# Within-chunk state-space kernels from a 32-column stationary operand, and the first loads in order of use

## The chip, the cores and the metric

One core of one Trainium2 chip runs the whole program. The metric is device time in microseconds (us), the median of several runs; less is better. The engines are TensorE (PE in the profile, its weight loads PEld), VectorE (DVE), ScalarE (ACT), GpSimd (POOL) and SyncE (SP, which here only sends DMAs). All work is in float32, or in pairs of float32r numbers that add up to one float32.

## What is computed

One layer of a hybrid encoder on a sequence of 512 tokens, width 2048, batch 1. The parts that the change touches are the input projection for `u` and the S5 scan; the rest is cut short.

```python
h = rmsnorm(x, norm_g)
v, bg, cg, za, u, zb, ga, gb = split(h @ w_in)      # 2048 -> 14336 columns
ya = (bg * causal_conv3(cg * v) * silu(za)) @ w_out_a
yb = gelu(s5_scan(u, ...))                          # 64 groups of 16 channels, 64 complex states each
yb = (yb * sigmoid(yb @ w_glu + b_glu) * silu(zb)) @ w_out_b
m = sigmoid(ga) * ya + sigmoid(gb) * yb
out = rmsnorm(x + m @ w_o, final_g)

# s5_scan, per group: lam_bar = exp(lam*dt); b_bar = (lam_bar-1)/lam * b
# h[l] = lam_bar * h[l-1] + b_bar @ u[l];  y[l] = Re(c @ h[l]) + d_skip * u[l]
```

## The kernel before

**Matrices.** Every large product is split: a float32 operand becomes a high part in float32r (an ACT cast, line 663 for weights, 734 for activations) and a low part (a DVE subtraction, line 680 for weights, 66 or 76 for activations), and PE sums hi·hi, hi·lo and lo·hi. The class `WStream` holds the order of all weight tiles: `_loads` sends the DMAs on the SP queue (line 641), `_hi` casts, `_lo` subtracts, `prep` does one weight's `_lo` and keeps the casts a little ahead, and `get` hands out the next pair after preparing up to two further ones. Most tiles in SBUF come from one pool of 37 slots, `r4`.

**Order of the stages.** First the projection for `u`: for each of 16 blocks k of 128 input channels, the block `x_k` (line 845) and the weight `w_k` (line 641) are loaded, `scale_x(k)` multiplies `x_k` by the norm's gain and splits it (line 893 on ACT, 76 on DVE), and 21 matmuls follow (lines 910 to 912). Squares for the norm (line 856) and, from k=2, steps of the state-space parameters (`ssm_params`, which loads them in line 91) go along. Then come the other projections, with the rest as background work. The list `bg` holds generators; after each product `step` runs some of them, so their instructions are written between the products. [...]

**The state-space blocks.** `ssm_blocks` treats the 64 groups in four blocks of 16 groups, 8 pairs each. A chunk is T = 4 steps, so there are 128 chunks in 512 tokens. The class `Block` has these stages:

- `loads`: the block's `u` in the layout [step and channel, chunk] (`u4`), and its parameters.
- `front`: `F`, the output matrix times powers of lam_bar for 0 to 4 steps (partitions are the 128 states of a pair of groups), and `bb`, the input matrix. Before, `bb` is two tiles of [128, 8 pairs, 4 steps, 2 groups, 16 channels], real and imaginary, in which the same 32 columns of a pair stand four times, once for each step. POOL clears them (line 344) and ACT fills them (line 347).
- `pe1`: line 376 gives each chunk's contribution to the states; lines 381 to 385 (shown in the profile as line 383) give the kernels within a chunk, `kp`: for each pair, `bb` is the stationary operand (128 states by 128 columns) and `F` for 0 to 3 steps the moving one (64 columns). `kp` therefore holds on each of four groups of 32 partitions the same numbers.
- `post`: copies the states' part out (line 394) and builds `mi`, the 128x128 matrix from the inputs of a chunk to its outputs: for step s, partitions 32s to 32s+31, the kernels for 0 to 3-s steps go to the outputs s to 3 (line 405, an ACT copy with the mask `msk`, which lets one group's 16 rows of every 32 through).
- `scan`: the recurrence over chunks on DVE; `pe2` (lines 484 and 487): outputs from `mi` and the states; `result` adds the skip part and writes to `uy`.

After the four blocks `gelu` forms the inputs of the GLU product. From there to the end come the GLU, both output projections (with products of 2x2 blocks in seven instead of eight multiplications, lines 1067 and 1072) and the last projection (line 1290).

Of the kernel before, what the change touches and what calls it, by code (L numbers as in the profile page):

```python
# [12 lines left out]
AF = mybir.ActivationFunctionType  # L13
# [3 lines left out]
P = 128  # L17
L = 512
D = 2048
KD = D // P  # L20
NG, NP, NC = 64, 64, 16
NQ = NG // 2
NB = 4
QB = NQ // NB
T = 4
# [55 lines left out]
def ssm_params(c, par, scratch):  # L81
# [3 lines left out]
    nc = c.nc  # L85
    tt, ts, stt = _ew(nc)
    W = 96
    a_t = c.r4.tile([P, 3, W], F32, tag="r4", name="ssm_par")
    keep = c.r4.tile([P, 14, 2, NQ], F32, tag="r4", name="ssm_keep")
    pw, up, coef, mag = keep[:, 0:5], keep[:, 5:12], keep[:, 12], keep[:, 13, 0]  # L90
    nc.gpsimd.dma_start(a_t, par)
    views = []

    def new():
        if not views:
            blk = c.r4.tile([P, 10, W], F32, tag="r4", name="ssm_tmp")
            views.extend(blk[:, i, :] for i in range(9, -1, -1))
        return views.pop()
# [94 lines left out]
    p1r, p1i, t = new(), new(), new()  # L193
# [51 lines left out]
    bt = c.r4.tile([P, 2, NQ, 8], F32, tag="r4", name="ssm_bt")  # L245
# [27 lines left out]
class Block:  # L273
# [32 lines left out]
    def front(self):  # L306
        c, nc, b, q0, msk = self.c, self.c.nc, self.b, self.q0, self.msk
        tt, ts, stt = _ew(nc)
        smal, wb, bs = self.smal, self.wb, self.bs

        self.F = []
        cr, ci = smal[:, :, 1, 0, :], smal[:, :, 1, 1, :]
        shp = [P, QB, NC]
        ft = self.new([P, QB, 5, NC], "ft")
        sh5 = [P, QB, 5, NC]
        p5 = [c.pw[:, :, i, q0:q0 + QB].rearrange("p t q -> p q t").unsqueeze(3).to_broadcast(sh5)
              for i in range(2)]
        c5 = [v.unsqueeze(2).to_broadcast(sh5) for v in (cr, ci)]
        for ri in range(2):
            f = self.new(sh5, "f")  # L320
            tt(ft, c5[1], p5[1 - ri], MUL)
            tt(f, c5[0], p5[ri], MUL)
            yield
            if ri == 0:
                tt(f, f, ft, SUB)
            else:
                fl = f.rearrange("p q t c -> p (q t c)")
                stt(fl, fl, -1.0, ft.rearrange("p q t c -> p (q t c)"), MUL, SUB)
            self.F.append(f)
            yield  # L330

        br, bi = smal[:, :, 0, 0, :], smal[:, :, 0, 1, :]
        kr = c.coef[:, 0, q0:q0 + QB].unsqueeze(2).to_broadcast(shp)
        ki = c.coef[:, 1, q0:q0 + QB].unsqueeze(2).to_broadcast(shp)
        self.bb = bb = [self.new([P, QB, T, 2, NC], "bb") for _ in range(2)]
        bt = [ft[:, :, i, :] for i in range(4)]
        tt(bt[0], br, kr, MUL)
        tt(bt[1], bi, ki, MUL)
        tt(bt[2], br, ki, MUL)
        tt(bt[3], bi, kr, MUL)  # L340
        tt(bt[0], bt[0], bt[1], SUB)
        tt(bt[2], bt[2], bt[3], ADD)
        for ri in range(2):
            nc.gpsimd.memset(bb[ri], 0.0)
            for g2 in range(2):
                hp = slice(g2 * 64, (g2 + 1) * 64)
                nc.scalar.copy(bb[ri][hp, :, :, g2, :],
                               bt[2 * ri][hp].unsqueeze(2).to_broadcast([64, QB, T, NC]))
        yield

        self.sl = []
        tmp = self.new([P, QB, 2, NP], "t")
        for ri in range(2):
            if ri == 0:
                tt(tmp, wb, bs, MUL)
                tt(tmp[:, :, 0, :], tmp[:, :, 0, :], tmp[:, :, 1, :], SUB)
            else:
                tt(tmp[:, :, 0, :], wb[:, :, 0, :], bs[:, :, 1, :], MUL)
                tt(tmp[:, :, 1, :], wb[:, :, 1, :], bs[:, :, 0, :], MUL)
                tt(tmp[:, :, 0, :], tmp[:, :, 0, :], tmp[:, :, 1, :], ADD)  # L360
            yield
            m = self.new([P, QB, 2, NP], "sl")
            for g2 in range(2):
                nc.scalar.activation(m[:, :, g2, :], tmp[:, :, 0, :], AF.Copy, scale=msk[:, g2:g2 + 1])
            self.sl.append(m)
            yield

    def pe1(self):
        c, nc = self.c, self.c.nc
        self.hp = []  # L370
        for ri in range(2):
            for half in range(2):
                ps = c.psum()
                for i in range(4):
                    q = half * 4 + i
                    nc.tensor.matmul(ps[:, i * NCH:(i + 1) * NCH],  # L376
                                     self.sl[ri][:, q].rearrange("p g s -> p (g s)"),
                                     self.u4[:, q, :], start=True, stop=True)
                self.hp.append(ps)
        kp = self.kp = c.psum()  # L380
        for q in range(QB):
            for ri in range(2):
                nc.tensor.matmul(kp[:, q * 64:(q + 1) * 64],  # L383
                                 self.bb[ri][:, q].rearrange("p t g c -> p (t g c)"),
                                 self.F[ri][:, q, 0:T].rearrange("p t c -> p (t c)"),
                                 start=ri == 0, stop=ri == 1)

    def post(self):
        c, nc, msk = self.c, self.c.nc, self.msk
        self.hs = []  # L390
        for ri in range(2):
            h = self.new([P, QB, NCH], "h")
            for half in range(2):
                nc.scalar.copy(h[:, half * 4:half * 4 + 4, :].rearrange("p q k -> p (q k)"),
                               self.hp[ri * 2 + half])
            self.hs.append(h)
            yield

        mi = self.mi = self.new([P, QB, T, 2, NC], "mi")
        nc.gpsimd.memset(mi, 0.0)  # L400
        kv = self.kp.rearrange("p (q t c) -> p q t c", t=T, c=NC)
        for s in range(T):
            hp = slice(s * 32, (s + 1) * 32)
            for g2 in range(2):
                nc.scalar.activation(mi[hp, :, s:T, g2, :], kv[hp, :, 0:T - s, :], AF.Copy,
                                     scale=msk[hp, g2:g2 + 1])
            if s % 2:
                yield

        self.el = []  # L410
        for ri in range(2):
            e = self.new([P, QB, T, 2, NC], "el")
            nc.gpsimd.memset(e, 0.0)
            for g2 in range(2):
                hp = slice(g2 * 64, (g2 + 1) * 64)
                nc.scalar.copy(e[hp, :, :, g2, :], self.F[ri][hp, :, 1:5, :])
            self.el.append(e)
            yield
# [278 lines left out]
def hybrid_kernel(ctx: ExitStack, tc: tile.TileContext, xT, x, cvec, fg, wu, wu7, wabc,  # L697
                  wgz, wgb, wga, wo, par, bs_d, be_d, ce_d, out):
    nc = tc.nc
    tt, ts, stt = _ew(nc)  # L700
    act = nc.scalar
    c = Ctx()
# [26 lines left out]
    def pair():  # L729
        t = c.r4.tile([P, 2, L], F32R, tag="r4", name="pair")  # L730
        return t
# [5 lines left out]
    W = WStream(c, 2, 2)  # L737
# [20 lines left out]
    for j in range(0, KD, 2):  # L758
        for i in range(4):
            W.add7(wabc[j, i, 0], wabc[j + 1, i, 0], wabc[j + 1, i, 1], wabc[j, i, 1])  # L760
        i = NAB + j - 2
# [18 lines left out]
    bgl, dsk, msk = cv_t[:, 64:72], cv_t[:, 72:104], cv_t[:, 104:106]  # L780
# [60 lines left out]
    def load_x(k):  # L841
        if k % 2 == 0:
            xt = c.r4.tile([P, 2, L], F32, tag="r4", name="xt")
            xs.extend([xt[:, 0], xt[:, 1]])
        nc.sync.dma_start(xs[k], xT[:, k])
# [13 lines left out]
    hp = []  # L859
# [27 lines left out]
    def scale_x(k):  # L887
        if k < KD:
            xg = pair()
            if k == 0:  # L890
                ts(xg[:, 0], xs[k], ng[:, k:k + 1], MUL)
            else:
                act.activation(xg[:, 0], xs[k], AF.Copy, scale=ng[:, k:k + 1])
            stt(xg[:, 1], xs[k], ng[:, k:k + 1], xg[:, 0].bitcast(F32), MUL, SUB)
            xgs.append(xg)

    load_x(0)
    W._loads(0)
    load_x(1)
    load_x(2)  # L900
    for k in range(KD):
        for i in range(2 * k + 3, min(2 * k + 5, KD)):
            load_x(i)
        xg = xgs.pop(0)
        hi, lo = W.get()
        for i in ((1, 2) if k == 0 else (k + 2,)):
            scale_x(i)
        for m in range(7):
            cs = slice(m * P, (m + 1) * P)
            nc.tensor.matmul(pu[m], hi[:, cs], xg[:, 0], start=k == 0, stop=False)  # L910
            nc.tensor.matmul(pu[m], hi[:, cs], xg[:, 1], start=False, stop=False)  # L911
            nc.tensor.matmul(pu[m], lo[:, cs], xg[:, 0], start=False, stop=k == KD - 1)  # L912
        for i in range(2 * k, min(2 * k + 2, KD)):
            square(i)
        if k >= 8:
            for _ in range(2):
                next(nrm, None)
        elif k >= 2:
            step(PRATE)
# [63 lines left out]
    for m in range(8):  # L983
        ps = psum()
        gemm(ps, yg)
        th, g = tmp(), tmp()
# [150 lines left out]
    for j in range(0, KD, 2):  # L1137
# [7 lines left out]
        i = NAB + j - 2  # L1145
# [40 lines left out]
    for j in range(NP7):  # L1186
# [5 lines left out]
        g, t = (v[:, j % 2] for v in mq[j // 2])  # L1192
# [322 lines left out]
```

## Time and profile before

| | |
|---|---|
| median of 3 runs | 1662.81 us (1661.98 to 1663.66) |
| the profiled execution | 1664.87 us, span 1663.1 us |
| PE busy | 1648.4 us, 99% of the span |
| DVE, ACT, POOL busy | 1289.0, 793.3, 226.5 us |
| matmuls of line 383 | 128 records, from 165.6 to 335.7 us |
| the first stage, 0 to 20 us | PE busy 16.51 us, DMA at 338 GB/s |

[...] A float32 matmul stands as two records. A wait is put down to the instruction that came last by the profile. "Idle before" stands in brackets behind a timeline row, with what ended it.

### The profile page before, as it was taken

The page shows a single profiled execution, that of the slowest core. Times are in us where ns is not written, and L with a number is a line of the kernel's source. Part 1 is how long each engine was busy: PE and PEld are TensorE (multiplying, and loading weights), DVE is VectorE, ACT ScalarE, POOL GpSimd, SP SyncE. Part 2 cuts the span into 40 slices and gives each one's busy share as a digit, 9 for nine tenths or more (in the row PEclk, how much of TensorE's full clock was granted, in tenths as well). Part 3 has the DMA queues.
Part 4 walks back from the last instruction along what each step waited for, and adds up shares of the span by engine and source line. Part 5 has one row for each costly group of instructions (what it writes and reads, how often), then busy time and mean ns, then how long its engine had stood idle before and what let it go on. Part 6 is the DMA issues. An engine that isn't in the chain of part 4 may idle for free.

```text
span 1663.1 us, 22776 instructions
## 1 busy us (share of the span) xinstructions
PE 1648.4 (99%) x8636; PEld 1415.5 (85%) x8636; DVE 1289.0 (78%) x1743; ACT 793.3 (48%) x1081; POOL 226.5 (14%) x352
## 2 busy tenths in 40 slices
PE   9999999999999999999999999999999999999997
PEld 7888888888888888888888888888888888888886
DVE  7897787885765687877778777777878688888497
ACT  6434455446422355545445555544545544445334
POOL 0003332200021100110110101001010221122000
PEclk9999999999999999999999999999999999999999
DMA  8323453442364567777777777777676888997683
GB/s 308 106 90 113 121 151 118 137 134 77 124 224 133 165 180 204 189 202 206 206 202 183 205 194 199 206 194 219 181 211 181 293 260 240 272 324 250 231 328 101
DMA packets 91822, 318.50 MB, mean 192 GB/s; under 512 B 11904, under 2 KB 12032, under 8 KB 91712
## 3 DMA queue, kind: packets, MB, share of 16 engines
q1 hardware_dynamic: 58608, 204.50, 35.7%
q0 software_dynamic: 32384, 111.45, 28.6%
q8 instruction: 67, 1.10, 0.3%
q10 hardware_dynamic: 720, 1.10, 0.2%
q14 instruction: 43, 0.35, 0.1%
HBM read 287.51 MB, written 25.30 MB: 188 GB/s over the span
## 4 chain that ended last, share of the span: by engine, by line
PE 91%; DMA 3%; DVE 2%; ACT 2%; issue 1%; POOL 0%; SPq 0%; DVEq 0%; ACTq 0%; POOLq 0%
PE ps L1067 33%; PE ps L1072 17%; PE ps L1290 9%; PE ps L835 8%; PE ps L834 8%; PE ps L833 8%; DMA h_sum<-yag 2%; PE ps L910 1%; PE ps L911 1%; PE ps L912 1%; PE ps L376 1%; PE ps L383 1%; PE ps L487 1%; DMA uy<-ssm_y 1%; DMA w_raw<-in_wga_dram 0%
## 5 line engine op out<-in xcount | busy, mean ns | idle before, releaser
L663 ACT CAST w_hi<-w_raw 128x1024 fp32r<-128x1024 f32 (+2 forms) x459 | 479.0, 1044 | 664.0 <-PE ps L1067 269.8
L680 DVE TENSOR_TENSOR w_lo<-w_raw,w_hi 128x1024 fp32r<-128x1024 f32 (+2 forms) x459 | 556.4, 1214 | 180.0 <-ACT w_hi L663 176.9
L1067 PE MATMUL ps<-h_comb,w_hi 128*128 128x512 f32 x1408 | 352.7, 392 | 0.8 <-DVE half L66 0.8
L1067 PEld LDWEIGHTS ps<-h_comb,w_hi 128*128 128x128 f32 x1408 | 253.2, 189 | 46.3 <-DVE half L66 1.0
L833 PE MATMUL ps<-pair,w_hi 128*128 128x512 f32 x720 | 281.1, 391 | 0.6 <-ACT pair L734 0.5
L835 PE MATMUL ps<-pair,w_lo 128*128 128x512 f32 x720 | 280.6, 390 | 0.7 <-DVE w_lo L680 0.7
L834 PE MATMUL ps<-pair,w_hi 128*128 128x512 f32 x720 | 280.4, 390 | 0.5 <-DVE pair L66 0.5
L1067 PE MATMUL ps<-pair,w_hi 128*128 128x512 f32 x1056 | 264.4, 392 | 0.0
L1067 PEld LDWEIGHTS ps<-pair,w_hi 128*128 128x128 f32 x1056 | 190.1, 189 | 34.1
L1072 PEld LDWEIGHTS ps<-h_comb,w_lo 128*128 128x128 f32 x1408 | 192.1, 190 | 13.7
L1072 PE MATMUL ps<-h_comb,w_lo 128*128 128x256 f32 x1408 | 196.3, 282 | 0.0
L835 PEld LDWEIGHTS ps<-pair,w_lo 128*128 128x128 f32 x720 | 135.2, 188 | 29.2 <-DVE w_lo L680 1.5
L834 PEld LDWEIGHTS ps<-pair,w_hi 128*128 128x128 f32 x720 | 135.2, 188 | 28.9 <-DVE pair L66 1.2
L833 PEld LDWEIGHTS ps<-pair,w_hi 128*128 128x128 f32 x720 | 135.2, 188 | 28.8 <-ACT pair L734 1.4
L1072 PEld LDWEIGHTS ps<-pair,w_lo 128*128 128x128 f32 x1056 | 144.1, 190 | 10.3
L1072 PE MATMUL ps<-pair,w_lo 128*128 128x256 f32 x1056 | 147.2, 282 | 0.0
L66 DVE TENSOR_TENSOR half<-ps,half 128x512 f32<-128x512 f32 x132 | 90.6, 687 | 67.6 <-PE ps L1072 67.6
L647 POOL DMA_DIRECT2D w_raw<-in_wabc_dram x64 | 55.0, 860 | 554.5 <-DMA w_raw<-in_wabc_dram 291.7
L1290 PE MATMUL ps<-w_hi,pair 128*128 128x512 f32 x192 | 60.8, 389 | 0.0
L567 DVE TENSOR_TENSOR w_raw<-w_raw 128x1024 f32<-128x1024 f32 x44 | 53.9, 1225 | 5.6 <-DMA w_raw<-in_wga_dram 4.3
L571 DVE TENSOR_TENSOR w_raw<-w_raw 128x1024 f32<-128x1024 f32 x44 | 53.9, 1225 | 1.5
L1290 PE MATMUL ps<-w_hi,m_half 128*128 128x512 f32 x160 | 50.8, 389 | 0.0
(216 smaller groups left out, 1743.6 us busy)
## 6 DMA issues: line engine op xcount, KB each, us to landing
w_raw<-in_wabc_dram SPq DMA_DIRECT2D x160, 512.0 KB, 4.4
w_raw<-in_wga_dram SPq DMA_DIRECT2D x76, 512.0 KB, 5.1
w_raw<-in_wabc_dram POOLq DMA_DIRECT2D x64, 512.0 KB, 6.5
w_raw<-in_wo_dram SPq DMA_DIRECT2D x52, 512.0 KB, 5.7
w_raw<-in_wgb_dram SPq DMA_DIRECT2D x48, 512.0 KB, 3.6
w_raw<-in_wgz_dram SPq DMA_DIRECT2D x24, 512.0 KB, 3.9
w_raw<-in_wga_dram POOLq DMA_DIRECT2D x24, 512.0 KB, 7.6
m_r<-m POOLq DMA_DIRECT2D x32, 256.0 KB, 5.7
```

Of the source, the lines that this page charges most:

```text
L66: return v.tensor_tensor(out=o, in0=a, in1=b, op=op)
L567: tt(out=b11["x"], in0=b11["x"], in1=s1["x"], op=ADD)
L571: tt(out=s1["x"], in0=b12["x"], in1=b11["x"], op=ADD)
L647: nc.gpsimd.dma_start(box["x"], src.rearrange("p a b -> p (a b)"), accum_op=ADD)
L663: nc.scalar.copy(hi[:, a:b], raw[:, a:b])
L680: nc.vector.tensor_tensor(out=lo[:, a:b], in0=raw[:, a:b], in1=hi.bitcast(F32)[:, a:b], op=SUB)
L833: nc.tensor.matmul(ps, hi[:, k], a[:, 0], start=first and k == 0, stop=False)
L834: nc.tensor.matmul(ps, hi[:, k], a[:, 1], start=False, stop=False)
L835: nc.tensor.matmul(ps, lo[:, k], a[:, 0], start=False, stop=last and k == 7)
L1067: nc.tensor.matmul(ps if flat else both, hi[:, k], a, start=first and k == 0, stop=False, skip_group_check=True)
L1072: nc.tensor.matmul(ps[:, HL:], lo[:, k], a[:, :HL] if flat else a[:, 0], start=False, stop=last and k == 7, skip_group_check=True)
L1290: nc.tensor.matmul(ps, l, r[:, k2, c0:c1], start=first and k2 == i == 0, stop=last and k2 == 1 and i == 2, skip_group_check=True)
```

## The change

Three edits.

1. `bb` becomes one tile of [128, 8 pairs, 2 (real, imaginary), 2 groups, 16 channels], without the four copies. The matmuls of `pe1` have 32 stationary columns instead of 128 and write 32 partitions of PSUM. In `post` the copy for each step s reads these 32 partitions and writes partitions 32s to 32s+31.
2. The first loads go x0, w0, x1, w1, x2, w2, x3, w3 instead of x0, w0, x1, x2, x3, x4, w1 and so on, and the first calls of `_hi`, `_lo`, `scale_x` and `prep` are written out ahead of the loop, so that `scale_x(1)` comes ahead of the cast of w1.
3. The state-space parameters are sent from the SP queue instead of POOL's, at the same place in the code.

```diff
-    nc.gpsimd.dma_start(a_t, par)
+    nc.sync.dma_start(a_t, par)
...
-        self.bb = bb = [self.new([P, QB, T, 2, NC], "bb") for _ in range(2)]
+        self.bb = bb = self.new([P, QB, 2, 2, NC], "bb")
...
+        nc.gpsimd.memset(bb, 0.0)
         for ri in range(2):
-            nc.gpsimd.memset(bb[ri], 0.0)
             for g2 in range(2):
                 hp = slice(g2 * 64, (g2 + 1) * 64)
-                nc.scalar.copy(bb[ri][hp, :, :, g2, :],
-                               bt[2 * ri][hp].unsqueeze(2).to_broadcast([64, QB, T, NC]))
+                nc.scalar.copy(bb[hp, :, ri, g2, :], bt[2 * ri][hp])
...
-        kp = self.kp = c.psum()
+        kp = self.kp = c.psum()[0:32]
         for q in range(QB):
             for ri in range(2):
                 nc.tensor.matmul(kp[:, q * 64:(q + 1) * 64],
-                                 self.bb[ri][:, q].rearrange("p t g c -> p (t g c)"),
+                                 self.bb[:, q, ri].rearrange("p g c -> p (g c)"),
                                  self.F[ri][:, q, 0:T].rearrange("p t c -> p (t c)"),
...
-                nc.scalar.activation(mi[hp, :, s:T, g2, :], kv[hp, :, 0:T - s, :], AF.Copy,
-                                     scale=msk[hp, g2:g2 + 1])
+                nc.scalar.activation(mi[hp, :, s:T, g2, :], kv[:, :, 0:T - s, :], AF.Copy,
+                                     scale=msk[0:32, g2:g2 + 1])
...
-    load_x(0)
-    W._loads(0)
-    load_x(1)
-    load_x(2)
+    for k in range(4):
+        load_x(k)
+        W._loads(k)
+    W._hi()
+    W._lo()
+    scale_x(1)
+    W.prep()
+    scale_x(2)
     for k in range(KD):
-        for i in range(2 * k + 3, min(2 * k + 5, KD)):
+        for i in range(2 * k + 4, min(2 * k + 6, KD)):
             load_x(i)
         xg = xgs.pop(0)
         hi, lo = W.get()
-        for i in ((1, 2) if k == 0 else (k + 2,)):
-            scale_x(i)
+        if k:
+            scale_x(k + 2)
```

## The prediction

> **What bounds the kernel now.** I read four views: the page's busy line and chain, the waits of TensorE (PE), then two stretches of the timeline, the first 25 us and the stretch round one small-state-space (SSM) block, because the diff touches only those two places.
>
> ```profile
> PE 1648.4 (99%) x8636; PEld 1415.5 (85%) x8636; DVE 1289.0 (78%) x1743; ACT 793.3 (48%) x1081; POOL 226.5 (14%) x352
> ...
> PE 91%; DMA 3%; DVE 2%; ACT 2%; issue 1%; POOL 0%; SPq 0%; DVEq 0%; ACTq 0%; POOLq 0%
> ```
>
> ```profile
> PE ps L910 <- ACT pair L893: 1.7, 1, 1.7
> PE ps L791 <- DVE bgl L785: 1.1, 1, 1.1
> PE ps L1067 <- DVE half L66: 0.8, 1, 0.8
> PE ps L835 <- DVE w_lo L680: 0.7, 1, 0.7
> PE ps L910 <- ACT w_hi L663: 0.6, 1, 0.6
> PE ps L833 <- ACT pair L734: 0.5, 1, 0.5
> PE ps L834 <- DVE pair L66: 0.5, 2, 0.3
> ```
>
> The columns of the waits are total, times, longest. PE is busy 99% of the span and waits less than 6 us in all, of which 2.3 us are on L910 in the first stage. So a microsecond taken from PE's own instructions, or from its wait on L910, is a microsecond of the kernel, unless another chain is just behind. VectorE (DVE, 78%) is the one that could be; I come back to it.
>
> **Part 1: the kernels within a chunk (line 383).** Each of the four SSM blocks issues 16 float32 matmuls here, each shown as two records, after 16 of line 376.
>
> ```profile
> 163.81 1.95 PE L376 MATMUL ps<-ssm_u,ssm_sl 128*128 128x128 f32 x16
> 165.59 3.68 PE L383 MATMUL ps<-ssm_f,ssm_bb 128*128 128x64 f32 x32
> 169.08 0.48 PE L834 MATMUL ps<-pair,w_hi 128*128 128x512 f32 x1
> 169.39 0.40 PE L835 MATMUL ps<-pair,w_lo 128*128 128x512 f32 x1
> 169.63 0.39 PE L833 MATMUL ps<-pair,w_hi 128*128 128x512 f32 x1
> 169.86 0.39 PE L834 MATMUL ps<-pair,w_hi 128*128 128x512 f32 x1
> ```
>
> ```profile
> L383 PEld LDWEIGHTS ps<-ssm_f,ssm_bb x128: 192/192/192, 165.5 to 335.7; 128*128 128x128 f32 x128
> L383 PE MATMUL ps<-ssm_f,ssm_bb x128: 222/275/275, 165.6 to 335.7; 128*128 128x64 f32 x128
> ```
>
> ```profile
> 51.73 0.86 PE ps L863 x2
> 52.59 0.23 PE ps L910
> ```
>
> Durations overlap, so I go from start to start. Line 376: (165.59 - 163.81)/16 = 0.111 us a record with 128 moving columns. Line 383: (169.08 - 165.59)/32 = 0.109 us a record with only 64. Line 863, the one float32 matmul with 512 moving columns, takes 0.86/2 = 0.43 us a record in the chain of waits; that scales to 0.107 for 128 columns and 0.054 for 64. So line 376 runs at its streaming time and line 383 at twice its own: something that did not shrink with the moving columns holds it, and what both lines share is a stationary operand of 128 columns. The change cuts that operand to 32 columns, with the same number of matmuls and moving columns.
>
> No row of this trace has a narrow stationary operand, so I bound the new period. Best end: 0.054, the streaming time, 128 x (0.109 - 0.054) = 7.0 us gained over the four blocks. No-gain end: 0.109 stays, if what holds it is a fixed cost of a load and matmul pair. A loss is not excluded (rival C). I take 0.060, near the streaming end, because line 376 shows pairs running at their streaming time with only 0.004 on top, so no fixed cost beside the larger of the two bounds is seen at that size. That is 128 x 0.049 = 6.3 us. Entering and leaving a run of different matmuls costs something already: after the float32 group the gap from L834 to L835 is 0.31 us instead of 0.23. I charge 0.1 at each side of four blocks for the changed width, 0.8 us. Net 5.5 us.
>
> [...]
>
> The other engines in this part. ScalarE (ACT) copies of line 347 shrink from 512 to 128 elements; POOL clears half as much.
>
> ```profile
> L405 ACT ACTIVATE ssm_mi<-ps,cvec_t 32x512 f32<-32x512 f32 (+3 forms) x32 | 14.9, 512 | 3.1 <-PE ps L383 3.0
> L347 ACT COPY ssm_bb<-ssm_ft 64x512 f32<-64x512 f32 x16 | 9.8, 616 | 0.1
> L344 POOL MEMSET ssm_bb<- 128x1024 f32 x8 | 7.5, 968 | 7.3 <-DVE ssm_h L66 5.7 <-DVE w_lo L680 1.6
> ```
>
> At most 9.8 us of ACT and 7.5 us of POOL in all go, from engines that are 48% and 14% busy; nothing waits for them, so I cost both at nothing. The 32 copies of line 405 now read 32 PSUM partitions and write another 32. No row shows such a shift. Lower bound: unchanged at 512 ns. Upper: twice, 14.9 us more on ACT over four blocks. Their results are wanted by line 484 of the next block step; in the last block they start at 339.6 and line 484 at 371.3 (rows below), so some 30 us of other matmuls cover either value.
>
> **Part 2: the first loads.** Before, the SyncE queue (SP) sends x0, w0, x1 to x4, then w1 to w5. After, x0, w0, x1, w1, x2, w2, x3, w3, and the second input is scaled ahead of the casts of w1 and w2.
>
> ```profile
> 6.72 0.72 ACT L663 CAST w_hi<-w_raw 128x640 fp32r<-128x640 f32 x1 [2.15 <-DMA w_raw<-in_wu_dram]
> 7.39 2.64 ACT L856 ACTIVATE tmp<-xt 128x512 f32<-128x512 f32 x4
> 10.53 0.94 ACT L663 CAST w_hi<-w_raw 128x896 fp32r<-128x896 f32 x1 [0.51 <-DMA w_raw<-in_wu_dram]
> 11.68 0.94 ACT L663 CAST w_hi<-w_raw 128x896 fp32r<-128x896 f32 x1 [0.20 <-DMA w_raw<-in_wu_dram]
> 12.52 0.72 ACT L893 ACTIVATE pair<-xt,cvec_t 128x512 fp32r<-128x512 f32 x1
> ```
>
> ```profile
> 11.22 0.39 PE L912 MATMUL ps<-pair,w_lo 128*128 128x512 f32 x1
> 13.29 0.50 PE L910 MATMUL ps<-pair,w_hi 128*128 128x512 f32 x1 [1.69 <-ACT pair L893]
> ```
>
> ```profile
> 0.00:20.00 20.00, 16.51 (x68) 12.95 (x69) 11.05 (x18) 13.81 (x21) 0.88 (x5) 1.00 0.92 338
> ```
>
> (The last row: the window, then busy time of PE, weight loads, DVE, ACT, POOL, granted clock, DMA share, GB/s.) The stream's period is 0.227 us (169.63 to 169.86 above, rounded), so step k=1 could have begun at 11.22 + 0.23 = 11.45; it began at 13.29, because the scaled input (12.52) stood behind the casts of w1, which landed at 10.53, and w2, 11.68. With x2 to x4 (3 x 256 KB) out of its way, w1 lands 0.79 MB / 338 GB/s = 2.3 us sooner, at 8.2; its cast ends at 9.2 and its low part, one 1.1 us DVE subtraction, at 10.3. The scaled x1 no longer waits for w2. All this is before 11.45, so the 1.84 us go whole. What is late next is w2, wanted at 11.45 + 21 x 0.227 = 16.2 and landing near 10.3 (704 KB more): no new wait.
>
> The parameter load (144 KB) leaves POOL's queue, where it was sent at 1.3, and goes to SP, where by the code it stands behind x0 to x9 and w0 to w7. Its share of the early bandwidth, 0.15 MB / 338 GB/s = 0.44 us, falls in front of w0's second piece, which PE waited 0.6 us for (L910 on w_hi). I take 0.2 us of it, bounds 0 and 0.44. With 0.1 us for the thinner issue of k=1's first matmuls, part 2 gives 2.1 us (1.6 to 2.4).
>
> The cost side of that move: 6.3 MB ahead of the parameters at 338 GB/s put their landing near 19 us. Their first reader on DVE:
>
> ```profile
> 19.58 1.08 DVE L680 TENSOR_TENSOR w_lo<-w_raw,w_hi 128x896 fp32r<-128x896 f32 x1
> 20.58 0.75 DVE L76 SCALAR_TENSOR_TENSOR pair<-xt,cvec_t,pair 128x512 fp32r<-128x512 f32 x1
> 21.24 0.69 DVE L66 TENSOR_TENSOR ss<-ss,tmp 128x512 f32<-128x512 f32 x1
> 21.85 0.20 DVE L72 TENSOR_SCALAR ssm_tmp<-ssm_par 128x96 f32<-128x96 f32 x1
> ```
>
> Shifted by 2 us, the reader comes at 19.8, 0.8 us after the landing. If it is late, DVE stands still, and queued behind it are squares' sums and the next low parts. The one made at 19.58 is the sixth weight's (k=5) while PE is in k=2 (from 13.29 + 4.77 = 18.1), so two stages, about 9.5 us, cover a late parameter load. I cost it at nothing. POOL has nothing else to do then; on SP it is one issue more in a queue that itself waits for earlier loads.
>
> **Does the gain reach the end?** The place where another chain is closest behind PE is the end of the SSM blocks.
>
> ```profile
> 362.15 2.36 DVE L66 TENSOR_TENSOR ssm_h<-ssm_h,ssm_t 128x1024 f32<-128x1024 f32 x2
> ...
> 376.83 0.69 DVE L66 TENSOR_TENSOR ssm_y<-ps,ssm_y 128x512 f32<-128x512 f32 x1 [1.99 <-PE ps L487]
> ```
>
> ```profile
> 371.27 0.38 PE L484 MATMUL ps<-ssm_u,ssm_mi 128*128 128x128 f32 x2
> ```
>
> The last block's states are ready at 364.5 and PE uses them at 371.3: 6.8 us of slack. If DVE did not move at all, 7.6 us less on PE would turn 0.8 us into a wait. DVE does move: its low parts wait for buffers that PE frees. After 376.8 the gelu chain hangs on PE's own output, so it and the matmuls beside it shift together, and PE's two short waits there (L833, L834, 1.0 us) stay.
>
> **The sum.** 5.5 + 2.1 = 7.6 us. Against the profiled execution's own 1664.87 us (span 1663.1 and 1.8 around it) that is 1657.3; this execution stands 2.1 us above the median of the three runs, 1662.81, so as a median 1655.2.
>
> **Rivals.** A: the narrow operand buys nothing, since the 0.109 belongs to the pair and not to the columns. For it: no row shows any pair below 0.106. Against it: that equals the streaming time there. Then only the loads count: 1662.8 - 2.1 = 1660.7, inside 0.2% (3.3 us, about what a measurement of this kernel can tell from no change). [...]
>
> B: the start is given back. ACT serves four squares at 7.39 whenever it is free; if they now land ahead of w1's cast, 2.6 us of ACT return the wait on L910. Then only part 1 counts: 1662.8 - 5.5 = 1657.3. Against it: those squares ran in an idle gap that earlier weights close.
>
> C, the other side: a load of 32 columns cannot run beside the matmul before it, so each record pays load and matmul in turn, 192 + 222 ns = 0.41 us instead of 0.109. That is 128 x 0.30 = 39 us lost, 1662.8 + 39 - 2.1 = 1699.7. It turns the sign once the period exceeds 0.109 + 2.1/128 = 0.125 us. Against it: loads run beside matmuls on every other line (PEld busy 85%, PE 99%). [...]
>
> **How the numbers follow.** Forecast 0.78, A 0.11, B 0.05, C with any worse stall of the same size class 0.06. Faster: forecast and B, 0.83; same: A, 0.11; slower: C, 0.06. The forecast's own range: part 1 from 3.7 (a period of 0.080, the 0.054 of streaming and a quarter of 0.109 for an unhidden load) to 7.0, part 2 from 1.6 to 2.4, so 1653.4 to 1657.5. The range given takes in A and B and leaves out C: 1653.2 to 1661.0.
>
> **What would show it.** Part 1: line 383's group of 32 records ends within about 2.1 us of its start instead of 3.49, in all four blocks. Part 2: the first L910 of k=1 near 11.4, no L910 wait on the pair of line 893, w_hi of w1 cast near 8.2; the first reader of the parameters without a long wait. Carried through: the start of the first line-487 group of the last block and the last matmul both some 7 us earlier. Wrong: a period of 0.109 or over 0.125, or a new wait of PE on L912, L484 or L835 before 420 us.

## The result, and the profile after

The changed kernel takes 1653.82 us (median of 4 runs, 1653.42 to 1654.27) against 1663.24 us before: a ratio of 0.9944, 95% interval [0.9927, 0.9961], 9.4 us less. Run again later beside other kernels it took 1655.67 against 1661.89, ratio 0.9960 [0.9948, 0.9973], 6.2 us less. The forecast was 1655.2 and 7.6 us less.

The page's head and the waits of PE, after (in the changed file the first stage's matmuls are lines 916 to 918 and line 376 is 375):

```profile
span 1652.1 us, 22757 instructions
...
PE 1641.3 (99%) x8636; PEld 1409.8 (85%) x8636; DVE 1290.6 (78%) x1743; ACT 788.0 (48%) x1081; POOL 220.7 (13%) x347
```

```profile
PE ps L791 <- DVE bgl L785: 1.1, 1, 1.1
PE ps L835 <- DVE w_lo L680: 0.7, 1, 0.7
PE ps L916 <- ACT pair L893: 0.4, 1, 0.4
```

PE is still busy 99%; its waits fell from 5.9 to 2.2 us. The timeline of PE in the first SSM block, after, and the two records' own line:

```profile
162.02 1.95 PE L375 MATMUL ps<-ssm_u,ssm_sl 128*128 128x128 f32 x16
163.90 1.97 PE L383 MATMUL ps<-ssm_f,ssm_bb 128*32 128x64 f32 x32
165.80 0.50 PE L834 MATMUL ps<-pair,w_hi 128*128 128x512 f32 x1
...
166.14 0.39 PE L835 MATMUL ps<-pair,w_lo 128*128 128x512 f32 x1
```

```profile
L383 PEld LDWEIGHTS ps<-ssm_f,ssm_bb x128: 106/110/110, 163.9 to 328.0; 128*32 128x32 f32 x128
L383 PE MATMUL ps<-ssm_f,ssm_bb x128: 219/219/243, 163.9 to 328.0; 128*32 128x64 f32 x128
```

The group of 32 records takes 165.80 - 163.90 = 1.90 us instead of 3.49, 0.0594 us a record. The group ahead of it takes 0.10 longer (1.88 instead of 1.78), the gap behind it 0.34 instead of 0.31. From the first to the last of these rows it is 4.12 us, and 5.58 before: 1.46 a block, 5.8 us in four.

The start, ACT and then PE, after:

```profile
6.12 0.73 ACT L663 CAST w_hi<-w_raw 128x640 fp32r<-128x640 f32 x1 [1.51 <-DMA w_raw<-in_wu_dram]
...
9.29 0.94 ACT L663 CAST w_hi<-w_raw 128x896 fp32r<-128x896 f32 x1 [0.75 <-DMA w_raw<-in_wu_dram]
10.14 0.63 ACT L856 ACTIVATE tmp<-xt 128x512 f32<-128x512 f32 x1
10.67 0.71 ACT L893 ACTIVATE pair<-xt,cvec_t 128x512 fp32r<-128x512 f32 x1
```

```profile
10.62 0.39 PE L918 MATMUL ps<-pair,w_lo 128*128 128x512 f32 x1
11.43 0.96 PE L916 MATMUL ps<-pair,w_hi 128*128 128x512 f32 x3 [0.43 <-ACT pair L893]
```

k=1 begins at 11.43 instead of 13.29, and w0's second piece is cast at 6.12 instead of 6.72. The scale of x1 stands behind w1's cast and a square, not ahead of the cast as its place in the code suggests (why, no run shows); in this execution PE waits 0.4 us for it.

### The profile page after: what moved, and what is told of

Read it like the earlier page. It is cut to its first block, busy times and chain, and to the rows that moved or that the text cites. A ratio compares the mean times of both kernels' runs of the same rounds, so it can differ in the third digit from the quotient of the medians.

```text
span 1652.1 us, 22757 instructions
## 1 busy us (share of the span) xinstructions
PE 1641.3 (99%) x8636; PEld 1409.8 (85%) x8636; DVE 1290.6 (78%) x1743; ACT 788.0 (48%) x1081; POOL 220.7 (13%) x347
## 4 chain that ended last, share of the span: by engine, by line
PE 98%; DVE 1%; DMA 0%; ACT 0%; SPq 0%; issue 0%; DVEq 0%
PE ps L1073 34%; PE ps L1078 18%; PE ps L835 10%; PE ps L833 10%; PE ps L834 10%; PE ps L1296 10%; PE ps L916 1%; PE ps L917 1%; PE ps L918 1%; PE ps L375 1%; PE ps L487 1%; PE ps L383 0%; PE ps L484 0%; DMA w_raw<-in_wu_dram 0%; DVE uy L66 0%; DVE o L76 0%
## 5 line engine op out<-in xcount | busy, mean ns | idle before, releaser
L1073 PE MATMUL ps<-h_comb,w_hi 128*128 128x512 f32 x1408 | 352.6, 392 | 0.0
L1073 PEld LDWEIGHTS ps<-h_comb,w_hi 128*128 128x128 f32 x1408 | 253.2, 189 | 45.3
L835 PE MATMUL ps<-pair,w_lo 128*128 128x512 f32 x720 | 280.6, 390 | 0.7 <-DVE w_lo L680 0.7
L833 PE MATMUL ps<-pair,w_hi 128*128 128x512 f32 x720 | 280.9, 390 | 0.0
L834 PE MATMUL ps<-pair,w_hi 128*128 128x512 f32 x720 | 280.2, 389 | 0.0
L1073 PE MATMUL ps<-pair,w_hi 128*128 128x512 f32 x1056 | 264.4, 392 | 0.0
L1073 PEld LDWEIGHTS ps<-pair,w_hi 128*128 128x128 f32 x1056 | 190.1, 189 | 34.0
L835 PEld LDWEIGHTS ps<-pair,w_lo 128*128 128x128 f32 x720 | 135.2, 188 | 29.2 <-DVE w_lo L680 1.4
L834 PEld LDWEIGHTS ps<-pair,w_hi 128*128 128x128 f32 x720 | 135.2, 188 | 28.0
L833 PEld LDWEIGHTS ps<-pair,w_hi 128*128 128x128 f32 x720 | 135.2, 188 | 27.7
```

The lines of the kernel that those rows point to most:

```text
L833: nc.tensor.matmul(ps, hi[:, k], a[:, 0], start=first and k == 0, stop=False)
L834: nc.tensor.matmul(ps, hi[:, k], a[:, 1], start=False, stop=False)
L835: nc.tensor.matmul(ps, lo[:, k], a[:, 0], start=False, stop=last and k == 7)
L1073: nc.tensor.matmul(ps if flat else both, hi[:, k], a, start=first and k == 0, stop=False, skip_group_check=True)
```

## The experiments

**One part alone.** `e1_narrow` is the change without the new order of loads:

```diff
-        self.bb = bb = [self.new([P, QB, T, 2, NC], "bb") for _ in range(2)]
+        self.bb = bb = self.new([P, QB, 2, 2, NC], "bb")   # and what belongs to it; loads as before
```

> Only the 32-column operand; the loads stay in the order of before, the parameters on POOL. Theory 1 (the change is the sum of two independent savings on PE): line 383 runs at 0.059 us a record, 4 x 1.44 = 5.7 us less than before, so about 1657.5, and the two waits of the first GLU product (L833, L834, together 2 us with the gaps around them) stay as before, since what took them away in the changed kernel was only an earlier landing of the last block's outputs. Theory 2 (those waits went because this part frees ACT and POOL): 7.7 us less, about 1655.5, and no wait on L833 or L834. Theory 3 (the narrow operand helps only because the start was moved too): less than 4 us.

`e2_order` has only the new order, with the parameters still on POOL's queue, and `e3_order_par` the parameters on SP as well:

```diff
-    load_x(0); W._loads(0); load_x(1); load_x(2)
+    for k in range(4): load_x(k); W._loads(k)              # and the written-out calls; bb as before
```

> Only the order of the first loads, casts and scalings; the wide operand stays, the parameters stay on POOL. Theory 1: the first L910 of k=1 comes near 11.5 to 11.9 instead of 13.29, 1.4 to 1.9 us less than before, 1661.3 to 1661.8; line 383 unchanged at 3.49 us a block. Theory 2 (waits of the first GLU product went through the start): about 1659.5. Rival (start given back later, at the wait on w_lo near 98 us or at the GLU): 1663, the same as before.

> The whole second part: order of loads and parameters on the SP queue, with the wide operand. Theory 1: 0 to 0.5 us less than with the parameters on POOL, from w0's second piece, cast at 6.1 instead of 6.7: 1661.0 to 1661.6. Rival: the parameters land late (sent at 15.4, some 22) and hold DVE, 0.5 us or more slower than with POOL.

Against 1663.25 us of the kernel before: `e1_narrow` 1657.5, ratio 0.9965 [0.9952, 0.9977]; `e2_order` 1659.53, 0.9980 [0.9971, 0.9989]; `e3_order_par` 1659.11, 0.9980 [0.9971, 0.9989]. So the operand gives 5.75 us and the loads 4.1, and the two add up to 9.9, near the first 9.4; the second series' 6.2 is less, with 1.6 us of waits on a later step in its profile (L1073, below). Each part gains without the other, so theory 3 and the rival of a start given back fall. The medians of `e2_order` and `e3_order_par` differ by 0.4 us, the step of the parameters' queue, which the runs do not resolve. But the loads gave more than the 1.4 to 1.9 of theory 1. The 1659.53 of `e2_order` is the number of its theory 2, yet the two waits of the first GLU product are gone in `e1_narrow` too, whose start is the old one, so the new start is not what took them away.

**The kernel before, profiled again.**

> The kernel before, profiled a second time. Theory 1 (the waits of the first GLU product are how the last block's outputs happened to land, 10.4 us after their issue, in one execution): they are shorter or gone here, the landing nearer 8 us, and the time some 2 us less than the first profile's 1664.9. Theory 2 (the waits belong to the kernel before, and every part of the change removes them): 1.0 us of waits on L833 and L834 again, landing above 10 us.

It took 1663.48. Its waits:

```profile
PE ps L910 <- ACT pair L893: 1.7, 1, 1.7
PE ps L791 <- DVE bgl L785: 1.1, 1, 1.1
PE ps L1067 <- DVE half L66: 1.0, 1, 1.0
PE ps L835 <- DVE w_lo L680: 0.7, 1, 0.7
PE ps L910 <- ACT w_hi L663: 0.6, 1, 0.6
```

The rows of L833 and L834 are missing: these waits come and go with the execution. The block's last outputs (first the profile shown in the prediction, then this one) were sent at the same point and read by the first gelu copy at:

```profile
390.42 1.12 ACT L937 COPY tmp<-uy 128x512 f32<-128x512 f32 x1 [7.27 <-DMA uy<-ssm_y]
```

```profile
388.87 1.13 ACT L937 COPY tmp<-uy 128x512 f32<-128x512 f32 x1 [5.51 <-DMA uy<-ssm_y]
```

That is 12.3 and 10.6 us after the first of them was issued (378.10 and 378.30), 10.1 in the changed kernel. Theory 1 of these waits holds: the same output was read 1.7 us sooner after its issue in one execution than in the other, and PE waited only in the other; the whole execution took 1.4 us less, where theory 1 had some 2. Likewise the wait of about 1 us on the combining step (L1067, later L1073) is in both profiles of before and in some of the changed kernel's: 1.6 us in the profile of its second series, none in its first. With a wait that size in kernels of both kinds and absent in others of both kinds (`e7_alt_wide` below, a variant of the kernel before, has none), it belongs to no part of the change.

**Why the start gave more.** The profile of `e1_narrow`, with the old order, shows what the two of the kernel before do not. PE's timeline:

```profile
13.36 1.56 PE L912 MATMUL ps<-pair,w_hi 128*128 128x512 f32 x5 [1.93 <-ACT pair L893]
14.72 0.63 PE L913 MATMUL ps<-pair,w_hi 128*128 128x512 f32 x1
15.14 0.63 PE L914 MATMUL ps<-pair,w_lo 128*128 128x512 f32 x1
15.57 0.63 PE L913 MATMUL ps<-pair,w_hi 128*128 128x512 f32 x1
...
18.04 0.39 PE L913 MATMUL ps<-pair,w_hi 128*128 128x512 f32 x1
```

The busy times by windows of `e1_narrow`, then the same windows of the kernel before (the eighth figure, before the DMA share, is the granted clock):

```profile
13.00:15.00 2.00, 1.64 (x6) 1.34 (x7) 2.00 (x3) 2.00 (x4) 0.00 (x0) 0.87 1.04 399
15.00:18.00 3.00, 3.00 (x8) 2.33 (x8) 3.00 (x5) 2.77 (x5) 0.00 (x0) 0.51 1.05 397
```

```profile
13.00:15.00 2.00, 1.71 (x7) 1.35 (x8) 2.00 (x3) 2.00 (x4) 0.00 (x0) 1.00 1.05 402
15.00:18.00 3.00, 3.00 (x14) 2.44 (x13) 3.00 (x5) 2.71 (x5) 0.00 (x0) 1.00 1.05 398
```

After the wait of 1.9 us on k=1's scaled input the granted clock fell to 0.51 from 15 to 18 us, and matmuls started every 0.43 us instead of 0.23. Counted in the trace from the first matmul (as 0), PE's record 100 started at 28.94 us here, at 27.30 and 27.48 in the two profiles of before, and between 24.6 and 25.7 in the ten profiles of kernels with the new order. `e7_alt_wide` (below), also with the old order, had the wait of 1.9 us, a clock of 0.59 in the same window and its record 100 at 28.83. So two of four executions with the old order lost about 1.5 us more to the clock, and none of those with the new order, which has no such gap.

What sets these executions apart can be read from the clock's own records. They begin at another time in each execution (4.26 us in `e1_narrow`, 7.22 in `e7_alt_wide`, 4.81 in the first profile of before, 6.81 in that of the changed kernel), and the changes of the clock read in these four stand a whole number of steps of 3.41 us after that: 3 and 4 steps in `e1_narrow`, 2 and 3 in `e7_alt_wide`, 484 and 481 in the other two. Windows laid on these steps, for `e1_narrow` (two), `e7_alt_wide` and the first profile of before (the third figure is PE's busy time):

```profile
11.08:14.50 3.42, 1.49 (x7) 0.86 (x5) 2.88 (x4) 3.24 (x5) 0.00 (x0) 1.00 1.02 403
14.50:17.91 3.41, 3.41 (x10) 2.72 (x9) 3.41 (x5) 3.27 (x6) 0.00 (x0) 0.50 1.06 399
```

```profile
10.63:14.05 3.42, 1.47 (x7) 0.87 (x7) 2.55 (x3) 3.23 (x5) 0.00 (x0) 1.00 1.03 411
```

```profile
11.64:15.05 3.41, 1.76 (x8) 1.37 (x9) 3.37 (x4) 3.38 (x5) 0.00 (x0) 1.00 1.04 408
```

PE stood idle for 1.93 and 1.95 us of one step in the two executions that lost the clock, and the next step ran at 0.50, from 14.50 to 17.91 us and from 14.05 to 17.46. In the first profile of before the idle time was 1.65, and in the second the whole wait was 1.70; both kept the clock at 1.00 up to 21 us. The ends of the programs fit: in the first profile of before the clock falls to 0.50 at 1656.86 us, after a step with 2.41 us of idle time, and in the changed kernel it stays at 1.00 after a step with 1.72 (from 1641.80 us) and falls at 1648.62, after one without any work of PE. So in these traces the clock fell after steps with 1.93 us of idle time and more, and not after those with 1.72 and less. Whether the place of a gap among the steps counts besides its length, no run shows.

The many other executions point the same way. A mean granted clock of 0.997 was recorded in 11 of 39 executions of the kernel before and in none of 49 with the new order; 0.998 and 0.999 occur in both. In the series of 21 the seven at 0.997 average 1663.9 us and the four at 0.999 1662.7.

**What holds a record of line 383.** `e4_two_copies` has 64 stationary columns, `e5_half_moving` 32 moving ones (it leaves out the kernels for 2 and 3 steps):

```diff
-        kp = self.kp = c.psum()[0:32]
+        kp = self.kp = c.psum()[0:64]                       # e4, with bb holding two copies
-                nc.tensor.matmul(kp[:, q * 64:(q + 1) * 64],
+                nc.tensor.matmul(kp[:, q * 64:q * 64 + 32], # e5, with F for 0 and 1 steps
```

> The changed kernel with two copies in 64 stationary columns instead of one in 32. Theory A (a record takes the longer of streaming, 0.054, and a weight load of 0.00085 us a column): 64 columns load in 0.054, the period stays at 0.059 to 0.062 and the time at that of the changed kernel, 1653.8. Theory B (load and streaming add up: 0.043 and 0.0005 a column, drawn through 0.109 and 0.059): 0.076, 1.9 us of group time becomes 2.4, some 2.1 us slower in all.

> The changed kernel with 32 moving columns instead of 64 in line 383, so the kernels for 2 and 3 steps are left out of the result. Theory A (the longer of streaming and load rules, and streaming is what is left at 0.059): streaming falls to 0.027 and the load of 32 columns is 0.027, so the period falls to 0.03 to 0.04; the group of 32 records takes about 1.0 to 1.3 us and all four blocks save 2.4 to 3.6 us. Theory C (0.059 is a fixed cost of a load and matmul pair): the period stays at 0.059, the time at 1653.8.

```profile
164.10 2.08 PE L384 MATMUL ps<-ssm_f,ssm_bb 128*64 128x64 f32 x32
166.11 0.50 PE L835 MATMUL ps<-pair,w_hi 128*128 128x512 f32 x1
```

```profile
163.11 1.20 PE L383 MATMUL ps<-ssm_f,ssm_bb 128*32 128x32 f32 x32
164.24 0.50 PE L834 MATMUL ps<-pair,w_hi 128*128 128x512 f32 x1
```

With 64 columns a record takes 2.01/32 = 0.063 us, near the changed kernel's 0.059 and far from the 0.076 of theory B; the time, 1655.65 in one run, holds a 1.0 us wait on the combining step and does not decide. With 32 moving columns it takes 1.13/32 = 0.035, so theory C, a fixed cost of the pair at 0.059, falls (1651.57 us in one run, with a 1.1 us wait on the combining step). An estimate fits these three shapes with 0.006 to 0.009 on top: the longer of streaming (0.43 us for 512 moving columns, line 863) and load (0.109 for 128 stationary columns, line 383 before), each scaled by its columns. It gives 0.054, 0.054 and 0.027 where 0.063, 0.059 and 0.035 were measured. The runs show that the period fell with the columns of the one operand and then of the other; that the first is the load is the author's reading.

**What a change of width costs.** `e6_alt_narrow` takes the matmuls of lines 375 and 383 in turn; `e7_alt_wide` does it in the kernel before, where the width is the same.

```diff
+                    q, ri = todo.pop(0)                     # after each matmul of line 375
+                    nc.tensor.matmul(kp[:, q * 64:(q + 1) * 64], ...)
```

> The changed kernel with the matmuls of lines 375 (128 stationary columns) and 383 (32) taken in turn, one each, so that the width changes some 32 times a block instead of twice. If a change of width costs 0.1 us, as I charged: about 30 x 0.1 x 4 = 12 us slower, 1666. If it drains the array (a matmul's 0.22 to 0.27 us less its period): up to 0.17 each, 20 us slower. If it costs nothing: 1654.

> The kernel before (128 stationary columns on both lines) with the matmuls of lines 376 and 383 in turn: the control for the alternation with 32 columns, which cost 0.32 us for each two changes of width (0.65 us for four records instead of 0.33). If the change of width is the cost: four records in 0.43 us here, and the time of before, 1663. If taking two kinds of matmul in turn is the cost: 0.65 us or more here too, some 15 us slower.

```profile
158.34 0.30 PE L381 MATMUL ps<-ssm_f,ssm_bb 128*32 128x64 f32 x2
158.57 0.49 PE L377 MATMUL ps<-ssm_u,ssm_sl 128*128 128x128 f32 x2
158.99 0.63 PE L381 MATMUL ps<-ssm_f,ssm_bb 128*32 128x64 f32 x8
```

```profile
168.21 0.33 PE L382 MATMUL ps<-ssm_f,ssm_bb 128*128 128x64 f32 x2
168.38 0.44 PE L378 MATMUL ps<-ssm_u,ssm_sl 128*128 128x128 f32 x2
168.66 0.33 PE L382 MATMUL ps<-ssm_f,ssm_bb 128*128 128x64 f32 x2
```

Two narrow and two wide records take 0.65 us where their periods add up to 0.33: 0.16 us for each change of width, as a mean of going in and out. Without a change of width the four take 0.45, their periods' 0.43. The order on the chip was not a strict alternation: the trace of `e6_alt_narrow` has 53 changes between the two lines in all, the changed kernel 4. The further 49 at 0.16 are 7.8 us; it took 1661.06, 7.2 more than the changed kernel's profiled 1653.86. `e7_alt_wide` took 1664.64, which is 1.2 us more than the second profile of the kernel before, and its record 100 alone came 1.4 us later, by the clock. The extra time stands at the changes, 0.16 us each, and not at each matmul as in rival C. The price is not fixed: in the changed kernel the two changes of a block, with 16 and 32 records between them, cost 0.13 us together.

**Four column strips at once.** `e8_col_tiles` writes the kernels of four successive pairs to four groups of 32 partitions:

```diff
-                nc.tensor.matmul(kp[:, q * 64:(q + 1) * 64],
+                nc.tensor.matmul(kp[q % 4 * 32:q % 4 * 32 + 32, q * 64:(q + 1) * 64],
...
+                for j in range(4):
+                    kr = slice(j * 32, (j + 1) * 32)
+                    nc.scalar.activation(mi[hp, j::4, s:T, g2, :], kv[kr, j::4, 0:T - s, :], AF.Copy,
+                                         scale=msk[kr, g2:g2 + 1])
```

> The changed kernel with the 8 pairs' kernels written in turn to four groups of 32 PSUM partitions, so that matmuls that follow each other use different column strips of the array; line 405 becomes 32 smaller ACT copies a block. If matmuls in different strips run at the same time: the group takes 0.5 to 1.0 us instead of 1.90, 3.6 to 5.6 us less, 1648 to 1650. If they still stream one after the other: 1653.8, the 24 further copies a block (some 5 us of ACT) being hidden as line 405 is now. If changing the strip costs like changing the width: 28 further changes a block at 0.1, some 11 us slower.

```profile
162.94 0.69 PE L383 MATMUL ps<-ssm_f,ssm_bb 128*32 128x64 f32 x32
163.56 0.50 PE L836 MATMUL ps<-pair,w_hi 128*128 128x512 f32 x1
```

The group takes 0.62 us, 0.019 a record: less than the streaming time of one (0.054), so strips do run together. 1650.78 us, ratio 0.9937 [0.9924, 0.9951], somewhat above the 1648 to 1650 expected; two of the five runs took 1654. A second series, beside the changed kernel, and the same with x1's high part on DVE (`if k <= 1` instead of `if k == 0` in `scale_x`):

> The changed kernel again, beside the two below on one chip. Theory 1: 1653.4 to 1654.3 as in its first runs; the first L910 of k=1 (now L916) between 10.6 and 11.6 depending on when w1 lands.

> The four-strip version again. The group of line 383 stays at 0.62 us a block, 5.1 us less than the changed kernel over four blocks, but its profile had 1.7 us of new waits (L375 on the ACT copies of ssm_sl 0.8, L489 on DVE's states 0.6, L836 0.3): 3.4 to 4 us less than the changed kernel, 1650 to 1650.5. Rival: two of its five runs were at 1654, as slow as the changed kernel; if that is its own behaviour, the median here may be near 1652.

> The four-strip version, with the high part of the second input x1 made on DVE, which is idle from 8.4 to 9.3, instead of on ACT, where it stands behind the cast of w1 and a square. If that scale is what k=1 waits for: its first matmul right after the last of k=0, 0.2 to 0.5 us less. If w1's own landing rules: no difference to the four-strip version.

On one chip: the changed kernel 1655.67, `e8_again` 1651.13, `e9_strips_dve` 1651.24; ratios to before 0.9960 [0.9948, 0.9973], 0.9931 [0.9918, 0.9945] and 0.9933 [0.9921, 0.9946]. The intervals of the strips lie just below that of the changed kernel beside them, so this version beats both kernels; none of the ten runs of it and of the variant on DVE stands at 1654 again. Of the 5.1 us that PE saves, some comes back as new waits in its second profile:

```profile
PE ps L375 <- ACT ssm_sl L363: 0.8, 1, 0.8
PE ps L837 <- DVE w_lo L682: 0.7, 1, 0.7
PE ps L489 <- DVE ssm_h L66: 0.6, 2, 0.3
```

New are the waits on L375 and L489, 1.4 us; L837 is the changed kernel's L835 by another number. The 128 smaller copies of line 405 (here L407) take 40.8 us of ACT where the 32 took 14.8, and the chains of ACT and DVE in the SSM blocks now reach PE. The scale of x1 on DVE made no difference to the time, but the test did not meet its case: w1's cast, which begins between 8.3 and 9.4 us from profile to profile, began at 8.39 there, and with it at 8.6 or earlier k=1 follows k=0 without a wait in every profile of the new order. Only in the two where it began at 9.29 and 9.41 did PE wait 0.4 us for the scaled x1.

## Why the prediction was right, and where not

- **Part 1's period** was the step that carried the forecast, 0.060 us; it measured 0.0594. The closeness is in part luck, since the prediction chose it between 0.054 and 0.109 with no narrow row at hand; the mechanism, not the digit, is what was reasoned. Entering and leaving cost 0.13 us a block instead of 0.2, so four blocks gave 5.8 us instead of 5.5, and `e1_narrow` alone 5.75. The reading behind it, that line 383 ran at its weight load and line 376 at its streaming, is an estimate that `e4_two_copies` (0.063 us a record) and `e5_half_moving` (0.035) agree with. Line 405's shift of partitions cost nothing, as its lower bound had it (510 ns a copy, before 512), and POOL clears a quarter of the elements, not half.
- **Part 2** was mis-sized: 2.1 us forecast, 4.1 measured by `e3_order_par`. That k=1 began at 11.43, as forecast (11.45), is luck: two misses cancel. k=0 ended 0.60 us sooner, since w0's second piece came 0.6 and not 0.2 earlier (its last matmul began at 10.62 instead of 11.22), and k=1 then waited 0.43 for the scaled x1, which does stand behind w1's cast; that cast began at 9.29 and not near 8.2. Where w1 came sooner there was no such wait, and k=1 began between 10.63 and 11.18.
- **What part 2 left out.** By record 100 the profiles of `e2_order` and `e3_order_par` are 2.3 to 2.8 us ahead of the two of before, neither of which lost the clock: so much is the start itself. Of the 4.8 us between the profiles of `b_again` and `e3_order_par`, a comparison record by record puts 2.8 there, 0.6 at the first GLU product and 1.3 at the combining step. Not in the sum at all was the clock, since the profile at hand did not show it: with the old order two of four traces lost some 1.5 us to it. How much of the medians' 4.1 is clock and how much the waits further on that come and go is not separated.
- **The total.** Two series of the changed kernel gave 9.4 and 6.2 us, on either side of the forecast 7.6. Their profiled executions differ by 1.8 us: record by record, the later one loses 2.1 at the waits on L1073 and is 0.6 ahead at the start. That the total lay in the range confirms part 1, not part 2.
- **The parameter load** landed at 15.4 + 6.5 = 21.9 us instead of 19, and its reader came at 24.70 instead of 19.8, since the order on DVE was laid out anew. With a reader at 19.8 it would have been late; the step "cost at nothing" held, in part by luck.
- **The two GLU waits** were said to stay. They were an accident of the profile of before, as `b_again` shows, and about 2 us of the profiled difference of 11.0 us lie there.
- **Carrying through** held: the last block's states were ready at 356.9 and used at 363.68, the same 6.8 us of slack as before, so DVE moved along with PE.

```profile
354.55 2.35 DVE L66 TENSOR_TENSOR ssm_h<-ssm_h,ssm_t 128x1024 f32<-128x1024 f32 x2
```

```profile
363.68 0.38 PE L484 MATMUL ps<-ssm_u,ssm_mi 128*128 128x128 f32 x2
```

- **Rivals.** A fell by the period: this narrow matmul alone, at 0.0594 us a record instead of 0.109, was 1.8 times as fast. B fell by `e3_order_par`. C fell by the period.

## What to carry to other kernels

Take the start-to-start distance of a matmul line and compare it with its streaming time, scaled from a long matmul of the same type; if it is longer, the stationary operand's columns may set it, as here (0.109 us a record with 128 columns, 0.0594 with 32, against 0.054), and loading only as many as the result needs is worth a try. Narrow results can then be put on different groups of 32 partitions; here their matmuls ran together, at 0.019 us a record. A gap of two microseconds on TensorE can cost more than itself: here two executions with a gap of 1.93 and 1.95 us lost some 1.5 us more, at a clock of 0.50, and the profile of the kernel before did not show that.

## What had not been expected of the hardware

The granted clock fell to 0.50 for 3.41 us after a wait of 1.9 us in the first stage, in two of four executions of the same start: those in which PE stood idle for 1.93 and 1.95 us of one step of 3.41 us, counted from the clock's first record. In the other two the wait was 1.69 and 1.70 us. In `e8_col_tiles` four strips of 32 columns ran float32 matmuls at 0.019 us a record, 3.1 times the rate of one strip (0.0594). A change of the stationary width cost 0.16 us where the two widths alternate every two records (`e6_alt_narrow`).
